# First block of a transformer trunk: three operand casts of the first turn are put in another order, and one product is issued in passes

## The chip, the cores and the metric

The kernel runs on one core of a Trainium2 chip, as one program with one launch. The metric is the device time of that program in microseconds (us); lower is better. A core has a matrix engine (PE), a vector engine (DVE), a scalar engine (ACT), GpSimd (POOL) and SyncE (SP). Each engine works through its own list of instructions in the order in which they were written, and waits on semaphores where an operand comes from another engine. Here SP starts the plain loads, and POOL starts the loads that add to what a tile holds already.

## The reference, cut to what matters

The trunk has two layers. The change lies in the very first block of the first layer, a SwiGLU feed-forward block on 512 tokens of width 1024, with 2816 hidden features:

```python
def swiglu_ffn(x, w_in, w_out):
    h = x @ w_in                       # (512, 1024) @ (1024, 5632)
    g, u = jnp.split(h, 2, axis=-1)
    return (jax.nn.silu(g) * u) @ w_out
...
x = layer_norm(a * x + 0.5 * swiglu_ffn(x, ffn_w_in[i, 0], ffn_w_out[i, 0]), ln_g[i, 0], ln_b[i, 0])
```

There are four such blocks in the program, two per layer; between them stand differential attention, a pooling mixer and two cross-attentions.

## The kernel before

**Products.** All products are made in float32 accuracy out of rounded parts: an operand is split into a high part (a cast on ACT) and a low part (source minus high part, on DVE), and a product of two split operands is three matmuls: high times high, low times high, high times low. `mm3` issues them one after the other for each block of 128 rows (lines 210, 211, 212 in the profile). `by_passes` (line 716) issues them in another order: first the sixteen matmuls that need only the high part of the weights, then the eight that need the low part.

**Seven products for eight.** The up projection works on units of 256 hidden columns. For one unit, the gate and the up half together with the two halves of the 1024 rows of the weights form a two by two block matrix; a Strassen-Winograd scheme makes it with seven block products instead of eight. The weights that these products need are sums of the blocks of `w_in`: they are made by loading a block into a buffer (`ra`, `rc`) and then letting POOL load another block on top with an adding DMA (`more`). The activations' sums ("factors") are made once per block by `second_factors`: factors 2 and 3 out of transposed x, then s2, s4 and s3, which are split into factors 4, 6 and 5 by `part`. "x's fourth sum" is s4: it becomes factor 6, the tiles `xe`.

**Units and turns.** `up` is a generator for one unit; its steps are, in order: x (factor 0), y (factor 1), z (factor 3, weights `ra` after one addition), z again (factor 6, accumulated into the same bank, weights `rd`, a second load into an `rc` buffer), then three products into x (factors 4, 5, 2). One product is 24 matmuls of 128x256. `ffn` runs three units in its first turn (lanes 0, 1, 2: first, second and third unit), calling `next` on each in a round; so the three z of factor 3 stand in a row, then the three z of factor 6, and so on. Later turns hold two units and a piece of the down projection each.

**Order.** Nothing reorders the instructions at run time: each engine's list follows the order in which the generators issue them, except where `issue_after` names an instruction that must come first; a casting instruction can then only be issued behind it. `operand(raw, behind)` does the casts of one weight block: the high part on ACT (line 689) behind `behind[0]`, the low part on DVE (line 691) behind `behind[1]`. At the start of the program (`at_start`) such ties are used because everything is short: x has to be loaded, transposed and split while the first weights land. There are four buffers each for the high (`wh`) and the low parts (`wl`) of weights; a buffer is reused when the matmuls that read it are done.

**Names in the profile.** `wh`, `wl` are weights' high and low part, `xh`, `xl`, `xe` factors' parts, `hb` and `sr` the sums before they are split, `sp` and `ha` copies of a bank that leave it free (p1, p5), `hr` the gated result. L760 and L761 are the add and the Silu on y, L772 the copy p5 of z, L125 and L126 the two instructions of `split`, L654, L656 and L661 the sums s2, s4 and s3.

Of the kernel before, what the change touches and what calls it, by code (L numbers as in the profile page):

```python
# [99 lines left out]
def drain(units):  # L100
    for _ in units:
        pass


def few(units, n):
    for _ in range(n):
        next(units, None)


class Trunk:  # L110
# [407 lines left out]
    def ffn(self, layer, j, ln, beside=()):  # L518
        w_in, w_out = self.a["ffn_w_in"][layer, j], self.a["ffn_w_out"][layer, j]
        self.seven_of, self.factors = {}, self.factor_tiles()  # L520
        nc, n, beside = self.nc, len(FFN_TURNS), iter(beside)
        at_start = bool(self.load_rest)
        downs = {i: self.down(d, w_out, 2.0 * ALPHA if i == 1 else 1.0) for i, (_, d) in enumerate(FFN_TURNS) if d}

        def start(turn):
            ups = FFN_TURNS[turn][0]

            early = (2, 1, 1) if turn == 0 else (0, 0)
            rest = self.load_rest.pop if turn == 0 and at_start else lambda: lambda: None
            got = [self.up(w_in, u, lane, early[lane], rest() if lane == 0 else None) for lane, u in enumerate(ups)]  # L530
            for lane, g in enumerate(got):
                next(g)
                if lane == 1:
                    rest()()
            if turn > 1:
                next(downs[turn])
            return got + [downs[i] for i in downs if i == turn]

        works = start(0)
        if at_start:  # L540

            zeros = self.act("hb", (P, P + S), mybir.dt.bfloat16)
            nc.vector.memset(zeros, 0.0)
            idle = self.aux("idle", "yz")
            self.warm(zeros, idle, 7)
            for tag, half in (("px", 0), ("py", 1)):
                for t in self.late[:2]:
                    self.turn(t, half, tag)
                if half == 0:
                    with self.tc.issue_after(self.last_turn.ins):  # L550
                        self.warm(zeros, idle, 9)
                next(works[0])
                if half == 0:
                    next(works[0])
            next(works[1])
        else:
            for w in works + works[:1]:
                next(w)
            self.turn_late(2)
        self.late = []  # L560
        next(works[0])
        act, dve = self.first_split
        if self.begins:

            for late, first in zip(self.begins, (act, dve)):
                self.queue_behind(late, first)
        second = self.second_factors()
        if at_start:

            next(works[0])  # L570
            for w in (works[1], second, second, works[1], works[2], works[2], works[0]):
                with self.behind():
                    next(w)
        else:
            for w in (second, *works[1:], second, downs[1]):
                next(w)
        for turn in range(n):
            behind = turn == n - 1
            for step in range(1 if turn == 0 else 0, 9 if behind else 7):
                if turn == 0 and step in (2, 3):  # L580
                    next(second)
                if step == 4:
                    if behind:
                        coming = [self.plain_down(w_out, layer, j, ln, beside)]
                    else:
                        coming = start(turn + 1)
                        if at_start and turn == 0:
                            with self.tc.issue_after(self.last_load.ins):
                                next(downs[1])
                if behind and step in (4, 6, 7, 8):  # L590
                    next(coming[0])
                if behind and step > 3:
                    few(beside, 2)

                for lane, w in enumerate(works[: None if not behind or step > 1 else -1]):
                    if not (at_start and turn == 0 and lane < 2 and step == 1):
                        next(w, None)
                if turn == 1 and step == 3:
                    self.seven_of[self.waiting[0]] = self.seven(self.waiting[1])
            works = coming  # L600
        drain(works[0])
# [13 lines left out]
    def second_factors(self):  # L615

        nc, F, H = self.nc, self.factors, 2 * P
        s1, a21, a11, a12 = (self.tmp("hb", (P, 4, H)) for i in range(4))  # L620
        s2 = self.tmp("sr", (P, 4, H))

        def sums():
            for r, (hi, lo) in zip((a11, a12), F):
                nc.vector.tensor_tensor(r, hi.bitcast(F32), lo.bitcast(F32), ALU.add)

        if self.begins is None:
            with self.tc.issue_after(self.second_split[1].ins):
                sums()

        def part(i, x, o=slice(0, H)):
            return self.split(F[i][0][:, :, o], F[i][1][:, :, o], x)

        for t in (2, 3):
            o = slice(t % 2 * P, (t % 2 + 1) * P)
            pts = []
            for half in range(2):
                pt = self.aux("pt", (("py", "yz"), ("px", "py"))[t % 2][half])
                pt = pt.rearrange("p (c n) -> p c n", c=4)
                c0 = half * S  # L640
                with self.behind():
                    self.transpose4(pt, [self.X[t][:, c0 + j * P : c0 + (j + 1) * P] for j in range(4)])
                pts.append(pt)
            nc.scalar.copy(a21[:, :, o], pts[0])
            if self.begins is None:
                self.turned_parts = part(2, pts[1], o)
            nc.vector.tensor_tensor(s1[:, :, o], pts[1], a21[:, :, o], ALU.subtract)
            self.made_parts = part(3, s1[:, :, o], o)
            if self.begins:
                part(2, pts[1], o)  # L650
            yield
        if self.begins:
            sums()
        nc.vector.scalar_tensor_tensor(s2, s1, -1.0, a11, ALU.mult, ALU.subtract)  # L654
        s4 = s1
        nc.vector.scalar_tensor_tensor(s4, s2, -1.0, a12, ALU.mult, ALU.subtract)  # L656
        part(6, s4)
        yield
        part(4, s2)
        s3 = a21  # L660
        nc.vector.tensor_tensor(s3, a11, a21, ALU.subtract)  # L661
        part(5, s3)
        yield

    def up(self, w, u, lane, early, between):
# [11 lines left out]
        def load(tag, *block):  # L677
            t = self.raw_tile((4, H), tag)
            self.last_load = nc.sync.dma_start(t, source(*block))
            return t  # L680
# [1 line left out]
        def more(t, *block):  # L682
            nc.gpsimd.dma_start(t, source(*block), accum_op=ALU.add)  # L683

        def operand(raw, behind=None):
            v = self.hl([P, 4, H])
            act, dve = behind or (None, None)
            with self.tc.issue_after(act.ins) if behind else nullcontext():
                hi = nc.scalar.copy(v[0], raw)  # L689
            with self.tc.issue_after(dve.ins) if behind else nullcontext():  # L690
                lo = nc.vector.tensor_sub(v[1], raw, v[0].bitcast(F32))  # L691
            splits.append((hi, lo))
            return v
# [28 lines left out]
        splits = []  # L722

        third = lane == 2
        at_start = early and self.begins is None
        sp = lambda: self.tmp("ha" if third else "sp", (P, 2, H))
        yz = "py" if third else "yz"
        ra = load("ra", 1, 1)
        if between:
            between()  # L730
        rc = load("rc", 2, 1)
        yield
        v = operand(ra, self.turned_parts if third and at_start else None)
        if early and lane == 0:
            self.first_split = splits[0]
        more(ra, 1, 2)
# [3 lines left out]
        if at_start and lane == 0:  # L740
            by_passes(x, v, 0, (0,))
            yield
        v2 = early > 1 and operand(rc, self.turned if at_start else None)
        if v2:
            self.second_split = splits[-1]
            yield
# [5 lines left out]
        nc.scalar.copy(p1, x)  # L752
        yield
        y = bank(self.aux("y", yz))
        v2 = v2 or operand(rc, self.made_parts if third and at_start else None)
        with self.behind() if at_start else nullcontext():
            product(y, v2, 1, True, lane != 1 and at_start)
        hr = self.tmp("hr", (P, 2, S))
# [1 line left out]
        nc.vector.tensor_tensor(h1, y, p1, ALU.add)  # L760
        nc.scalar.activation(h1, h1, AF.Silu)  # L761
        yield
        v = operand(ra, self.made_parts if at_start and lane == 0 else None)
        if at_start and lane == 0:
            self.made_parts = splits[-1]
            yield
        z = bank(self.aux("z", yz))
        product(z, v, 3, True)
        more(ra, 2, 2)
        rd = load("rc", 2, 2)  # L770
        p5 = sp()
        nc.scalar.copy(p5, z)  # L772
        yield
        product(z, operand(rd), 6)
        more(rd, 1, 2)
        yield
        product(x, operand(ra), 4)
# [911 lines left out]
```

## Time and profile before

| | |
|---|---|
| time, median of 3 runs | 1927.93 us (1924.76, 1927.93, 1930.44) |
| the profiled execution's own time | 1927.77 us |
| its span in the trace | 1926.0 us |
| PE busy | 1900.1 us, 99% of the span |
| DVE busy | 1564.4 us, 81% |
| ACT busy | 1022.8 us, 53% |
| POOL busy | 320.6 us, 17% |
| HBM traffic over the span | 143 GB/s |

The span is what the trace shows from the first to the last instruction of the profiled execution; its own time is 1.77 us longer, for what lies around it, and 0.16 us under the median of the three timed runs. A busy PE is counted from modelled ends of matmuls, so the idle times in front of single instructions and the start times tell more than the 99%. The start of the program is read in a timeline: one row for each instruction, with the start, the duration, the engine, the source line, what is written from what, and in brackets the idle time before it with what ended that.

### The profile page before, as it was taken

The numbers are of one execution on the slowest core, as the hardware profiler recorded it, in microseconds if no ns is written. First come the engines' busy times: TensorE is split into PE (matmuls) and PEld (weight loads), VectorE is DVE, ScalarE is ACT, GpSimd is POOL, SyncE is SP. The second block draws the span as 40 slices with busy tenths as digits, with TensorE's granted clock in tenths as the row PEclk, the third lists the DMA queues.
The fourth block names the chain that finished last, engine by engine and source line by source line (L and its number), as shares of the span: only waits on it lengthen the run. The fifth ranks groups of instructions, "written<-read, shape, count | busy, mean of one in ns | idle before, by whom it ended". The sixth has DMA issues, their size and how long they took to land.

```text
span 1926.0 us, 32482 instructions
## 1 busy us (share of the span) xinstructions
PE 1900.1 (99%) x13066; PEld 1741.3 (90%) x13066; DVE 1564.4 (81%) x2264; ACT 1022.8 (53%) x1580; POOL 320.6 (17%) x278
## 2 busy tenths in 40 slices
PE   9999999999999999999999999999999999999998
PEld 8999998888878888999998999999899889999997
DVE  7888989888967558888888988888887568998886
ACT  6555554567755435655554655455455436555553
POOL 2112121111210002211210321112130012111210
PEclk9999999999999999999999999999999999999999
DMA  9978772322124317978686588788344437877861
GB/s 236 220 170 184 167 141 86 91 66 88 55 99 153 110 66 192 181 175 164 139 192 179 105 179 171 176 164 186 111 132 132 132 88 157 182 160 170 184 133 56
DMA packets 246742, 277.94 MB, mean 144 GB/s; under 512 B 8256, under 2 KB 212544, under 8 KB 246592
## 3 DMA queue, kind: packets, MB, share of 16 engines
q0 software_dynamic: 92928, 92.29, 31.3%
q1 hardware_dynamic: 153664, 183.59, 29.7%
q8 instruction: 102, 1.67, 0.4%
q14 instruction: 48, 0.39, 0.1%
HBM read 273.75 MB, written 2.10 MB: 143 GB/s over the span
## 4 chain that ended last, share of the span: by engine, by line
PE 77%; DVE 14%; ACT 4%; issue 2%; DMA 2%; POOL 1%; SPq 0%; DVEq 0%; ACTq 0%; POOLq 0%
PE x L210 7%; PE x L211 7%; PE x L212 7%; PE z L212 4%; PE z L210 4%; PE z L211 4%; PE ps L210 3%; PE ps L212 3%; PE ps L211 3%; PE px L210 2%; PE px L212 2%; PE px L211 2%; PE y L212 2%; DVE wl L691 2%; PE xq L210 1%
## 5 line engine op out<-in xcount | busy, mean ns | idle before, releaser
L683 POOL DMA_DIRECT2D ra<-in_ffn_w_in_dram x132 | 171.3, 1318 | 988.9 <-DVE wl L691 812.2
L689 ACT CAST wh<-ra 128x1024 fp32r<-128x1024 f32 x176 | 185.0, 1053 | 215.6 <-PE x L211 66.6
L691 DVE TENSOR_TENSOR wl<-ra,wh 128x1024 fp32r<-128x1024 f32 x176 | 214.2, 1220 | 71.2 <-ACT wh L689 70.9
L689 ACT CAST wh<-rc 128x1024 fp32r<-128x1024 f32 x132 | 138.9, 1053 | 107.6 <-PE x L211 41.8
L210 PE MATMUL x<-xe,wh 128*128 128x256 f32 x704 | 195.2, 277 | 0.0
L211 PE MATMUL x<-xe,wh 128*128 128x256 f32 x704 | 195.1, 277 | 0.0
L212 PE MATMUL x<-xe,wl 128*128 128x256 f32 x704 | 195.0, 277 | 0.0
L125 ACT CAST wh<-b 128x1024 fp32r<-128x1024 f32 x112 | 117.8, 1052 | 132.3 <-PE x L211 65.6
L691 DVE TENSOR_TENSOR wl<-rc,wh 128x1024 fp32r<-128x1024 f32 x132 | 159.7, 1219 | 27.1 <-ACT wh L689 26.1
L126 DVE TENSOR_TENSOR wl<-b,wh 128x1024 fp32r<-128x1024 f32 x112 | 136.7, 1221 | 40.8 <-ACT wh L125 40.8
L210 PE MATMUL x<-xh,wh 128*128 128x256 f32 x536 | 148.9, 278 | 0.0
L211 PE MATMUL x<-xl,wh 128*128 128x256 f32 x536 | 148.5, 277 | 0.0
L212 PE MATMUL x<-xh,wl 128*128 128x256 f32 x536 | 148.5, 277 | 0.0
L211 PEld LDWEIGHTS x<-xe,wh 128*128 128x128 f32 x704 | 132.7, 189 | 1.4
L210 PEld LDWEIGHTS x<-xe,wh 128*128 128x128 f32 x704 | 132.2, 188 | 1.3
L212 PEld LDWEIGHTS x<-xe,wl 128*128 128x128 f32 x704 | 132.2, 188 | 0.0
L126 DVE TENSOR_TENSOR wl<-raw,wh 128x1024 fp32r<-128x1024 f32 x64 | 83.0, 1301 | 42.4 <-ACT wh L125 41.6
L211 PEld LDWEIGHTS x<-xl,wh 128*128 128x128 f32 x536 | 101.0, 189 | 0.7
L210 PEld LDWEIGHTS x<-xh,wh 128*128 128x128 f32 x536 | 100.6, 188 | 0.7
L212 PEld LDWEIGHTS x<-xh,wl 128*128 128x128 f32 x536 | 100.6, 188 | 0.0
L212 PE MATMUL z<-xe,wl 128*128 128x256 f32 x352 | 98.4, 280 | 2.2 <-DVE wl L691 2.2
L211 PE MATMUL z<-xe,wh 128*128 128x256 f32 x352 | 98.3, 279 | 0.4 <-DVE xe L126 0.4
(442 smaller groups left out, 6304.0 us busy)
## 6 DMA issues: line engine op xcount, KB each, us to landing
ra<-in_ffn_w_in_dram POOLq DMA_DIRECT2D x132, 512.0 KB, 7.0
rc<-in_ffn_w_in_dram SPq DMA_DIRECT2D x88, 512.0 KB, 5.7
b<-in_ffn_w_out_dram SPq DMA_DIRECT2D x76, 512.0 KB, 4.8
ra<-in_ffn_w_in_dram SPq DMA_DIRECT2D x44, 512.0 KB, 4.8
rc<-in_ffn_w_in_dram POOLq DMA_DIRECT2D x44, 512.0 KB, 7.9
raw<-in_xa_wkv_dram SPq DMA_DIRECT2D x16, 1024.0 KB, 5.4
raw<-in_da_w_qkv_dram SPq DMA_DIRECT2D x16, 512.0 KB, 5.3
raw<-in_xa_wq_dram SPq DMA_DIRECT2D x8, 1024.0 KB, 5.1
```

Source lines behind the costliest of these rows:

```text
L125: self.nc.scalar.copy(hi, src),
L126: self.nc.vector.tensor_sub(lo, src, hi.bitcast(F32)),
L210: mm(out, w[0], x[0], start=start, stop=False, skip_group_check=again)
L211: mm(out, w[0], x[1], start=False, stop=False, skip_group_check=again)
L212: self.last_mm = mm(out, w[1], x[0], start=False, stop=stop, skip_group_check=again)
L683: nc.gpsimd.dma_start(t, source(*block), accum_op=ALU.add)
L689: hi = nc.scalar.copy(v[0], raw)
L691: lo = nc.vector.tensor_sub(v[1], raw, v[0].bitcast(F32))
```

## The change

In the first turn of the first block (`at_start`), four things are different:

1. Lane 0 hands out an extra step for the second z: it issues the casts of `rd`, notes them in `made_parts` and yields. The loop in `ffn` takes that step (`next(works[0])`) when lane 1 has done step 2, so ahead of lane 2's z.
2. `second_factors` notes the split of s4 in `factor_parts`.
3. Lane 2's casts for its z of factor 3 are tied behind two pairs now: lane 0's `rd` casts and the split of s4. `operand` takes any number of such pairs.
4. Lane 2's z of factor 3 is issued by passes.

```diff
+                    if at_start and turn == 0 and lane == 1 and step == 2:
+                        next(works[0])
...
-        part(6, s4)
+        self.factor_parts = part(6, s4)
...
-        def operand(raw, behind=None):
+        def operand(raw, *behind):
             v = self.hl([P, 4, H])
-            act, dve = behind or (None, None)
-            with self.tc.issue_after(act.ins) if behind else nullcontext():
+            with self.after([act for act, _ in behind]):
                 hi = nc.scalar.copy(v[0], raw)
-            with self.tc.issue_after(dve.ins) if behind else nullcontext():
+            with self.after([dve for _, dve in behind]):
                 lo = nc.vector.tensor_sub(v[1], raw, v[0].bitcast(F32))
...
-        v = operand(ra, self.made_parts if at_start and lane == 0 else None)
-        if at_start and lane == 0:
+        if not at_start or lane == 1:
+            v = operand(ra)
+        elif third:
+            v = operand(ra, self.made_parts, self.factor_parts)
+        else:
+            v = operand(ra, self.made_parts)
             self.made_parts = splits[-1]
             yield
         z = bank(self.aux("z", yz))
-        product(z, v, 3, True)
+        product(z, v, 3, True, third and at_start)
         more(ra, 2, 2)
         rd = load("rc", 2, 2)
         p5 = sp()
         nc.scalar.copy(p5, z)
         yield
-        product(z, operand(rd), 6)
+        v = operand(rd)
+        if at_start and lane == 0:
+            self.made_parts = splits[-1]
+            yield
+        product(z, v, 6)
```

The other three blocks, the later turns of this one, and SP's list of loads keep their order. POOL's list changes in one place: the adding load of lane 0's `rc_484` stands ahead of that of lane 2's `ra_168` instead of behind it.

**DVE, around the s4 split, before.** `rc_484` is lane 0's `rd`, `ra_168` lane 2's weights for z, `rc_518` lane 1's `rd`; `hb_315<-sr_319,hb_318` makes s4, `xe_155` is the low part of factor 6, `xe_153` that of factor 4.

```order
L656 SCALAR_TENSOR_TENSOR hb_315<-sr_319,hb_318 128x1024
L691 TENSOR_TENSOR wl_523<-ra_168,wh_522 128x1024
L661 TENSOR_TENSOR hb_316<-hb_317,hb_316 128x1024
L126 TENSOR_TENSOR xe_155<-hb_315,xe_152 128x1024
L126 TENSOR_TENSOR xe_153<-sr_319,xe_150 128x1024
L691 TENSOR_TENSOR wl_562<-rc_484,wh_561 128x1024
L126 TENSOR_TENSOR xe_154<-hb_316,xe_151 128x1024
```

The same place of DVE now:

```order
L658 SCALAR_TENSOR_TENSOR hb_315<-sr_319,hb_318 128x1024
L692 TENSOR_TENSOR wl_523<-rc_484,wh_522 128x1024
L663 TENSOR_TENSOR hb_316<-hb_317,hb_316 128x1024
L126 TENSOR_TENSOR xe_155<-hb_315,xe_152 128x1024
L692 TENSOR_TENSOR wl_527<-ra_168,wh_526 128x1024
L126 TENSOR_TENSOR xe_153<-sr_319,xe_150 128x1024
L692 TENSOR_TENSOR wl_591<-rc_518,wh_590 128x1024
```

Lane 0's low part of `rd` has moved from fifth behind s4 to the place right behind it, and lane 2's low part has moved from there to behind the low part of factor 6.

**ACT, the same stretch, before.** `ha_416<-x_391` is lane 2's copy p1, `hr_451` its Silu, `sp_486<-z_458` and `sp_520<-z_492` the copies p5 of lanes 0 and 1.

```order
L752 COPY ha_416<-x_391 128x512
L689 CAST wh_522<-ra_168 128x1024
L689 CAST wh_561<-rc_484 128x1024
L761 ACTIVATE hr_451<-hr_451 128x2x256
L689 CAST wh_590<-rc_518 128x1024
L125 CAST xe_152<-hb_315 128x1024
L772 COPY sp_486<-z_458 128x512
L125 CAST xe_150<-sr_319 128x1024
```

And now:

```order
L753 COPY ha_416<-x_391 128x512
L690 CAST wh_522<-rc_484 128x1024
L762 ACTIVATE hr_451<-hr_451 128x2x256
L777 COPY sp_486<-z_458 128x512
L125 CAST xe_152<-hb_315 128x1024
L690 CAST wh_526<-ra_168 128x1024
L125 CAST xe_150<-sr_319 128x1024
L777 COPY sp_520<-z_492 128x512
L690 CAST wh_590<-rc_518 128x1024
```

Lane 0's cast comes first; lane 2's has gone from the first place behind p1 to behind lane 0's p5 and the high part of factor 6; lane 1's has gone behind lane 1's p5.

**PE, where lane 2's z of factor 3 (`z_530`) passes over to lane 0's z of factor 6 (`z_458`), now.** Before, the 24 matmuls of lane 2's product went in threes, each with `wl` as the third.

```order
L717 MATMUL z_530<-xh_85,wh_526 128x256
L717 MATMUL z_530<-xl_87,wh_526 128x256
L210 MATMUL z_458<-xe_152,wh_522 128x256
L717 MATMUL z_530<-xh_85,wl_527 128x256 x8
L211 MATMUL z_458<-xe_155,wh_522 128x256
L212 MATMUL z_458<-xe_152,wl_523 128x256
```

The eight matmuls with the low part now stand at the end of lane 2's product, behind the first matmul of lane 0's.

More of the change, by code (lines that the diff above doesn't have):

```diff
@@ L724, in up @@
         third = lane == 2
-        at_start = early and self.begins is None
+        at_start = early > 0 and self.begins is None
         sp = lambda: self.tmp("ha" if third else "sp", (P, 2, H))
@@ L732, in up @@
         yield
-        v = operand(ra, self.turned_parts if third and at_start else None)
+        v = operand(ra, *((self.turned_parts,) if third and at_start else ()))
         if early and lane == 0:
@@ L742, in up @@
             yield
-        v2 = early > 1 and operand(rc, self.turned if at_start else None)
+        v2 = early > 1 and operand(rc, *((self.turned,) if at_start else ()))
         if v2:
@@ L754, in up @@
         y = bank(self.aux("y", yz))
-        v2 = v2 or operand(rc, self.made_parts if third and at_start else None)
+        v2 = v2 or operand(rc, *((self.made_parts,) if third and at_start else ()))
         with self.behind() if at_start else nullcontext():
```

## The prediction

> **What bounds the kernel now.** I read the page first, for what is scarce over the whole span.
>
> ```profile
> PE 1900.1 (99%) x13066; PEld 1741.3 (90%) x13066; DVE 1564.4 (81%) x2264; ACT 1022.8 (53%) x1580; POOL 320.6 (17%) x278
> ```
>
> PE is the bound almost everywhere, so the change, which leaves out no work, can only give back time in which PE stands still or runs slowly, and only in the first turn of the first block, where it moves something. So next come the waits of PE over the first 130 us.
>
> ```profile
> PE z L212 <- DVE wl L691: 2.2, 1, 2.2
> PE z L211 <- DVE xe L126: 0.4, 1, 0.4
> ```
>
> Both stand at one place, the passage from the third unit's z (factor 3) to the first unit's z (factor 6). The timeline of PE there:
>
> ```profile
> 34.74 0.28 PE L210 MATMUL z<-xh,wh 128*128 128x256 f32 x1
> 35.15 0.38 PE L212 MATMUL z<-xh,wl 128*128 128x256 f32 x1
> 37.75 0.36 PE L210 MATMUL z<-xe,wh 128*128 128x256 f32 x1
> 38.51 0.38 PE L211 MATMUL z<-xe,wh 128*128 128x256 f32 x1 [0.40 <-DVE xe L126]
> 41.07 0.53 PE L212 MATMUL z<-xe,wl 128*128 128x256 f32 x1 [2.17 <-DVE wl L691]
> 41.40 0.42 PE L210 MATMUL z<-xe,wh 128*128 128x256 f32 x1
> 45.28 0.28 PE L210 MATMUL z<-xe,wh 128*128 128x256 f32 x1
> 48.00 0.28 PE L210 MATMUL z<-xe,wh 128*128 128x256 f32 x1
> ```
>
> The last two rows are the first matmuls of the second and the third unit's product: 24 matmuls in 48.00 - 45.28 = 2.72 us, 0.113 us each, undisturbed. The third unit's z took 37.75 - 34.74 = 3.01, which is 0.29 too long. The first unit's z of factor 6 took 45.28 - 37.75 = 7.53, which is **4.81** too long. Of that, 3.09 is waiting (its third matmul at 41.07 instead of 37.75 + 0.23 = 37.98) and 1.72 is slowness: from 41.40 on a matmul takes about 0.21 us. Two stretches of the busy-time table, with the granted clock third from the right, say why.
>
> ```profile
> 37.74:41.15 3.41, 0.83 (x5) 0.44 (x3) 3.21 (x4) 3.41 (x5) 0.00 (x0) 1.00 1.04 159
> 41.15:44.57 3.42, 3.42 (x16) 3.42 (x17) 3.42 (x4) 1.27 (x2) 2.04 (x2) 0.50 0.33 33
> ```
>
> After 3.41 us in which PE was busy for 0.83, the clock was granted at 0.50 for the next 3.42. So 0.29 + 4.81 = **5.10 us** is all that this place can give back. There is no other idle PE before 130 us that the change touches.
>
> Who makes PE wait is seen in the other engines' timelines. ACT:
>
> ```profile
> 27.80 0.57 ACT L752 COPY ha<-x 128x512 f32<-128x512 f32 x1
> 32.78 1.05 ACT L689 CAST wh<-ra 128x1024 fp32r<-128x1024 f32 x1 [4.41 <-DMA ra<-in_ffn_w_in_dram]
> 33.74 1.05 ACT L689 CAST wh<-rc 128x1024 fp32r<-128x1024 f32 x1
> 36.16 1.04 ACT L125 CAST xe<-hb 128x1024 fp32r<-128x1024 f32 x1
> 37.10 0.57 ACT L772 COPY sp<-z 128x512 f32<-128x512 f32 x1
> 37.58 1.04 ACT L125 CAST xe<-sr 128x1024 fp32r<-128x1024 f32 x1
> ```
>
> DVE:
>
> ```profile
> 30.91 1.22 DVE L656 SCALAR_TENSOR_TENSOR hb<-sr,hb 128x1024 f32<-128x1024 f32 x1
> 33.87 1.23 DVE L691 TENSOR_TENSOR wl<-ra,wh 128x1024 fp32r<-128x1024 f32 x1 [1.74 <-ACT wh L689]
> 37.23 1.22 DVE L126 TENSOR_TENSOR xe<-hb,xe 128x1024 fp32r<-128x1024 f32 x1 [1.01 <-ACT xe L125]
> 38.65 1.23 DVE L126 TENSOR_TENSOR xe<-sr,xe 128x1024 fp32r<-128x1024 f32 x1 [0.20 <-ACT xe L125]
> 39.80 1.22 DVE L691 TENSOR_TENSOR wl<-rc,wh 128x1024 fp32r<-128x1024 f32 x1
> ```
>
> ACT stood idle for 4.41 us for the third unit's accumulated weights, with the first unit's cast queued behind it, and then both engines made everything at once: the low part that PE waited for ended at 39.80 + 1.22 = 41.02.
>
> **The change part by part.** The new order is followed through with these durations. On a full engine the next large cast starts 0.95 after the last (ACT, 32.78 to 33.74), a small copy takes 0.48 of the queue (37.10 to 37.58), and a large DVE operation 1.15 at most (38.65 to 39.80), from which the times below are reckoned with 1.14.
>
> *The first unit's `rd` casts, moved ahead.* The high part can start when the load has landed. The issue in the window around 13.9 us, the lane 0 `rd`, and the time to landing:
>
> ```profile
> 13.90 0.37 SPq L679 DMA_DIRECT2D rc<-in_ffn_w_in_dram x1
> ...
> rc<-in_ffn_w_in_dram SPq DMA_DIRECT2D x1, 512.0 KB, 13.1
> ```
>
> It lands at 27.0, and its new `wh` buffer was last read by the third unit's x, long done. So the cast runs from about 28.3 to 29.3, in the idle time of ACT. On DVE the low part goes behind s4 (30.91), from 32.05 to 33.27. Both lie beside PE's z products of the first two units, at no cost: PE needs them at 37.5. What now stands behind the cast on ACT is the third unit's Silu, the first unit's p5 and the s4 split; the cover is 1.9 us, since p5 cannot start before the first unit's z ends.
>
> ```profile
> 31.91 0.28 PE L212 MATMUL z<-xh,wl 128*128 128x256 f32 x1
> ```
>
> *The s4 split, moved ahead.* p5 starts at about 32.23 (that matmul ends at 32.19), the high part of factor 6 at 32.71, until 33.75 (s4 itself is there at 32.13). On DVE: s3 from 33.18, then the low part from 34.32 to 35.54, where before it ended at 38.45. PE needs it at about 37.6. The 0.40 us wait is gone.
>
> *The third unit's casts, moved back.* They are what pays. The high part, now behind the split, starts at 33.67 instead of 32.78 and ends at 34.72. PE wants it at 34.74, when the second unit's z is issued. How PE takes up work after a cast is seen earlier in its timeline, where the cast ended at 26.42:
>
> ```profile
> 26.47 0.38 PE L716 MATMUL y<-xh,wh 128*128 128x256 f32 x1 [0.48 <-ACT wh L689]
> 26.69 0.28 PE L716 MATMUL y<-xl,wh 128*128 128x256 f32 x1
> ```
>
> 0.05 after the cast, and 0.11 lost on the first step. So PE starts at 34.77 and loses up to 0.14. The low part runs from 35.46 to 36.68 on DVE.
>
> *z by passes.* The 24 matmuls stay 24, but the low part is wanted only after 16 of them and the one of `z_458`, at 34.77 + 0.1 + 17 x 0.113 = 36.8, so 36.68 is in time by 0.1, where in threes it would have been wanted at 35.0. The 0.29 of before is gone; if DVE is late by d, d - 0.1 is lost.
>
> *What follows.* The third unit's `rd` is issued, and lands after, as these rows say:
>
> ```profile
> 28.15 0.37 SPq L679 DMA_DIRECT2D rc<-in_ffn_w_in_dram  x1
> ...
> rc<-in_ffn_w_in_dram SPq DMA_DIRECT2D x1, 512.0 KB, 7.6
> ```
>
> The first unit's z of factor 6 ends at about 40.3. The second unit's `rd` parts are made by 37.1 and 39.0, wanted at 40.3; the third's, landed at 35.75 and cast at 38, by 39.0 and 41.25, wanted at 43.0. The added waits of lane 2's casts hold back nothing that is wanted earlier than these. POOL's adding loads of the `rc` buffers are issued earlier, since their casts are; that of lane 0 goes ahead of that of lane 2's `ra`, behind a low part that is there at 33.3 instead of 41.0.
>
> *The sum.* Removed 5.10, added between 0 and 0.6 (0.14 for the start, the rest if both engines run half a microsecond behind this reckoning); I take 0.1, next to the reckoned row. The profiled execution's own time was 1927.77, so 1927.77 - 5.0 = **1922.8 us**, against the median of 1927.93 a saving of 0.26%. A measurement of this kernel can tell about 0.3%, 5.8 us, from no change.
>
> **The rivals.** *The slow clock was an accident of that execution.* The clock fell after a stretch of 3.41 us with little work, and where such stretches begin may differ between executions. The longest other single wait of PE, 1.36 us in the attention, left no trace in the granted clock, which is 1.00 all around it:
>
> ```profile
> 380.03 0.33 PE L494 MATMUL pt<-ident,p 128*128 128x128 f32 x1 [1.36 <-DVE p L1130]
> ...
> 376.00:392.00 16.00, 14.64 (x113) 13.96 (x113) 14.93 (x47) 10.63 (x29) 2.36 (x3) 1.00 0.13 44
> ```
>
> Here PE had two waits with one matmul between, some 2.6 us idle; cut by a border between two stretches, it might not have slowed PE, and then most executions before lost only 0.29 + 3.09 = 3.4. The gain is 3.3 and the time 1924.5. For it: the fastest of three runs is 3.2 under the median. Against: the profiled execution, with its slow stretch, lies at the median.
> [...]
>
> *The transfers keep their times.* The DMA engines are full up to the stall and nearly empty in it (second number from the right).
>
> ```profile
> 39.00:41.00 2.00, 0.00 (x0) 0.00 (x0) 2.00 (x3) 2.00 (x4) 0.00 (x0) 1.00 1.05 165
> 41.00:43.00 2.00, 1.93 (x9) 1.93 (x10) 2.00 (x3) 1.42 (x2) 1.28 (x1) 0.54 0.06 9
> ```
>
> If they stay full behind it, loads may land no earlier though PE is. The two casts that waited for a transfer later in this turn, and when PE wanted them:
>
> ```profile
> 65.19 1.05 ACT L689 CAST wh<-ra 128x1024 fp32r<-128x1024 f32 x1 [1.45 <-DMA ra<-in_ffn_w_in_dram]
> 71.38 1.05 ACT L689 CAST wh<-ra 128x1024 fp32r<-128x1024 f32 x1 [3.15 <-DMA ra<-in_ffn_w_in_dram]
> ```
>
> ```profile
> 72.48 0.28 PE L210 MATMUL x<-xh,wh 128*128 128x256 f32 x1
> 77.92 0.28 PE L210 MATMUL x<-xh,wh 128*128 128x256 f32 x1
> ```
>
> With PE 5.0 earlier they are wanted at 67.5 and 72.9. High parts end at 66.2 and 72.4, low parts 1.2 later, and those are wanted 0.2 after the start: no wait at the first, some 0.5 at the second. The gain would be 4.5 and the time 1923.3. It is unlikely in full, because the transfers paused for these two microseconds, at a share of 0.06, and now have something to do there.
>
> *Slower: the first unit's `rd` lands late and stands in front of everything on ACT.* The cast now heads ACT's list. If the load lands at T instead of 27.0, p5, the s4 split and the third unit's casts move by T - 30.7 as soon as T is over 30.7, and PE waits that long at 34.74, once more with a slow stretch of 1.7 behind it. The whole gain is used up from T = 34.0 on, and 1927.77 + 5.8 needs T near 40. For it: loads of this stretch take 7.6 to 13.1 us to land, all different. Against is the slowest load in the chain of waits, the third unit's first `rc`:
>
> ```profile
> 8.76 16.53 DMA rc<-in_ffn_w_in_dram
> ```
>
> With its 16.5 us T would be 30.4, just under the border; and nothing ahead of 27 us has moved. T at 40 gives about 1933.7.
>
> **How the numbers follow.** The forecast, -5.0, gets 0.78; the accident of the clock 0.11; the transfers 0.06; the late `rd` 0.05. The three runs lie within 5.7 us, so two medians differ by two or three microseconds by themselves: of the forecast, which is 0.8 short of the bound of 5.8, some two fifths (0.33) come out faster by over 0.3%; of the accident 0.03 and of the transfers 0.02. That is 0.38 faster; 0.05 slower, the late `rd` alone; the rest, 0.57, within 0.3%. The range goes from 1922.8 - 3.2 (the fastest run's distance from the median) = 1919.6 to the clock rival's 1924.5 with 2.0 of spread, 1926.5.
>
> **What would show it.** Right: no wait of PE over 0.2 us between 30 and 45 us; granted clock 1.00 throughout; the first unit's product of factor 6 ends near 40.3; ACT's first `rc` cast at 28.3; the product that began at 72.48 begins near 67.5. Wrong in size: a wait for `wh` at 34.7 or for `wl` at 36.8, or ACT waiting for a transfer after 60 us with PE idle behind it. Wrong altogether: ACT idle until after 30.7 for the first unit's `rd`, or a stretch at 0.50 somewhere else.

## The result and the profile after

The changed kernel takes **1923.05 us** (median of 13 runs, 1920.70 to 1926.82); the kernel before, run beside it, 1927.33 us (13 runs, 1924.76 to 1930.44). The ratio is 0.998 with a 95% interval of 0.9972 to 0.9989: 4.3 us less, with 2.1 to 5.4 inside the interval. The forecast was 1922.8. The execution that was profiled was the slowest of the 13: its own time is 1926.82, its span 1923.9 us. So places are compared here, not spans.

The waits of PE over the first 130 us of the changed kernel (in all, times, longest):

```profile
PE x L717 <- ACT wh L690: 1.3, 1, 1.3
PE idle L120 <- DVE hb L543: 1.2, 1, 1.2
PE y L717 <- ACT wh L690: 0.3, 1, 0.3
PE x L717 <- DVE wl L692: 0.3, 1, 0.3
```

There is no z among them any more. The same view of the kernel before has three waits beside the two z that the prediction showed:

```profile
PE idle L120 <- DVE hb L543: 1.3, 1, 1.3
PE y L716 <- ACT wh L689: 0.5, 1, 0.5
PE x L716 <- ACT wh L689: 0.2, 1, 0.2
```

So the waits that are left are of the kind that was there before. All four are earlier than the place in question. The first, at 24.00 us, is long in this execution, in which a load of weights came late (the cast that PE waited for began at 22.90, after ACT had stood idle for 2.19 us until that load, and in the profile of before at 21.22 without such a wait; in two more traces of this kernel the wait of PE is 0.2 us at most), and it is why everything below is some 1.45 us later than foretold. PE's timeline, from the third unit's z of factor 3 to the second unit's z of factor 6 and that of the third:

```profile
36.23 0.38 PE L717 MATMUL z<-xh,wh 128*128 128x256 f32 x1
36.45 0.28 PE L717 MATMUL z<-xl,wh 128*128 128x256 f32 x1
...
38.21 0.28 PE L210 MATMUL z<-xe,wh 128*128 128x256 f32 x1
38.40 1.22 PE L717 MATMUL z<-xh,wl 128*128 128x256 f32 x8
...
42.16 0.28 PE L210 MATMUL z<-xe,wh 128*128 128x256 f32 x1
...
44.99 0.28 PE L210 MATMUL z<-xe,wh 128*128 128x256 f32 x1
```

I call the time from the first of these rows to the row at 42.16 the **passage**: the 48 matmuls of two products, undisturbed 48 x 0.1133 = 5.44 us. Where PE's list mixes the products, the first 48 matmuls from the third unit's z on are counted, whichever product they belong to. It took 5.93 us here and 45.28 - 34.74 = 10.54 us in the profile of before. The busy-time table at the same place, with the granted clock third from the right:

```profile
33.58:36.99 3.41, 3.41 (x31) 3.36 (x30) 3.41 (x4) 3.31 (x4) 1.34 (x2) 1.00 1.15 189
36.99:40.41 3.42, 3.42 (x30) 3.31 (x30) 3.42 (x4) 3.42 (x6) 1.28 (x1) 1.00 1.24 197
40.41:43.82 3.41, 3.41 (x32) 3.41 (x31) 3.41 (x4) 2.52 (x4) 1.93 (x2) 1.00 1.24 198
```

PE and DVE are both busy throughout, and the clock stays at 1.00. ACT works in the new order, the first unit's `rd` (29.52) ahead of the split of s4 (34.17) and the third unit's weights (35.12), and without holes from the split on:

```profile
29.52 1.05 ACT L690 CAST wh<-rc 128x1024 fp32r<-128x1024 f32 x1
...
33.69 0.59 ACT L777 COPY sp<-z 128x512 f32<-128x512 f32 x1 [0.35 <-PE z L212]
34.17 1.05 ACT L125 CAST xe<-hb 128x1024 fp32r<-128x1024 f32 x1
35.12 1.05 ACT L690 CAST wh<-ra 128x1024 fp32r<-128x1024 f32 x1
```

and so does DVE (first unit's low part, the sum s3, low part of factor 6, third unit's low part):

```profile
33.72 1.22 DVE L692 TENSOR_TENSOR wl<-rc,wh 128x1024 fp32r<-128x1024 f32 x1
34.85 1.22 DVE L663 TENSOR_TENSOR hb<-hb 128x1024 f32<-128x1024 f32 x1
35.99 1.22 DVE L126 TENSOR_TENSOR xe<-hb,xe 128x1024 fp32r<-128x1024 f32 x1
37.13 1.21 DVE L692 TENSOR_TENSOR wl<-ra,wh 128x1024 fp32r<-128x1024 f32 x1
```

### The profile page after: what moved, and what is told of

It reads as the page before. It is cut to its first block, busy times and chain, and to the rows that moved or that the text cites. A ratio compares the mean times of both kernels' runs of the same rounds, so it can differ in the third digit from the quotient of the medians.

```text
span 1923.9 us, 32479 instructions
## 1 busy us (share of the span) xinstructions
PE 1899.5 (99%) x13066; PEld 1741.6 (91%) x13066; DVE 1563.9 (81%) x2264; ACT 1023.3 (53%) x1580; POOL 319.6 (17%) x278
## 4 chain that ended last, share of the span: by engine, by line
PE 78%; DVE 13%; ACT 4%; DMA 2%; issue 2%; POOL 1%; SPq 0%; DVEq 0%; ACTq 0%; POOLq 0%
PE x L210 7%; PE x L211 7%; PE x L212 7%; PE z L212 4%; PE z L210 4%; PE z L211 4%; PE ps L210 3%; PE ps L212 3%; PE ps L211 3%; PE px L210 2%; PE px L212 2%; PE px L211 2%; PE x L717 2%; PE y L212 2%; PE xq L210 2%
## 5 line engine op out<-in xcount | busy, mean ns | idle before, releaser
L125 ACT CAST wh<-raw 128x1024 fp32r<-128x1024 f32 x64 | 66.5, 1049 | 59.4 <-PE xq L211 21.2
```

The costliest lines, as they stand in the source:

```text
L125: self.nc.scalar.copy(hi, src),
```

## Experiments

The questions were: is it this place that pays; which part of the change pays; did the slow clock belong to the stall or to one execution; and would a late `rd` have cost what the rival said. Each run gives the passage from its trace, and most a time against the kernel before on the same chip. In g1 and g3, where PE stands still ahead of the passage, it is counted from the end of the second unit's last matmul instead, which makes it some 0.17 us shorter than the others' way of counting.

| kernel | passage, us | clock at it | time, us | before beside it |
|---|---|---|---|---|
| changed (three traces) | 5.93, 5.60, 5.78 | 1.00 | 1923.05 | 1927.33 |
| before (three traces) | 10.54, 11.59, 10.05 | 0.50 for 3.4, 6.8, 3.4 us | 1927.33 | |
| e1, `rd` first alone, with passes | 5.65 | 1.00 | 1924.20 | 1927.36 |
| e2, casts without passes | 5.98 | 1.00 | 1923.67 | 1927.36 |
| e3, passes alone | 10.40 | 0.50 for 3.4 us | 1927.64 | 1927.36 |
| e4, the wait filled | 8.43 | 1.00 | 1926.19 | 1927.36 |
| g2, tie to s4 and passes | 7.23 | 1.00 | 1924.94 | 1926.65 |
| g1, `rd` late | 7.02 | 1.00 | 1924.49 | 1926.65 |
| g3, `rd` later | 15.10 | 0.50 for 6.8 us | 1931.38 | 1925.76 |

**e1: the first unit's `rd` casts ahead, third unit's casts not tied to s4.** From the changed kernel:

```diff
-            v = operand(ra, self.made_parts, self.factor_parts)
+            v = operand(ra, self.made_parts)
```

> Measure D: from the first matmul of the third unit's z (factor 3) to the first matmul of the second unit's z of factor 6; 10.54 us in the trace before, 5.93 in the trace of the change, 5.44 without any stall. Here lane 0's rd casts stay ahead, and z stays in passes, but lane 2's casts are no longer tied behind the split of s4. Theory (the first unit's low part was late, and its move is what pays): the third unit's casts run first, the low part of factor 6 ends near 37.5, just when PE wants it, so D is 5.4 to 6.2, and the second unit's low part may cost another 0.5 one product later; time within 1 us of the changed kernel (1923). Rival (the tie behind s4 is what pays): D of 8 or more, time near 1926.

The passage, again from the third unit's z to the second unit's z of factor 6:

```profile
35.90 0.28 PE L717 MATMUL z<-xh,wh 128*128 128x256 f32 x1
...
41.55 0.28 PE L210 MATMUL z<-xe,wh 128*128 128x256 f32 x1
```

5.65 us, no wait, and not even the short start at the third unit's first matmul (0.28 where the changed kernel has 0.38); its cast is no longer tied behind the split of s4. The ratio to before is 0.9983 (0.9975 to 0.9992). The time of 1924.20 is 1.2 us over that of the changed kernel, where 1 was allowed, but the intervals of the two gains overlap. So the tie to s4, which moves the third unit's casts further back, adds nothing that can be seen once `rd` is ahead.

**e2: the casts in the new order, z not by passes.** From the changed kernel:

```diff
-        product(z, v, 3, True, third and at_start)
+        product(z, v, 3, True)
```

> All casts as in the changed kernel, but the third unit's z goes in threes again. Theory: its first low part is wanted 0.23 us after the start and comes about 1.9 us after it (DVE 35.46 to 36.68 in the reckoning), so PE waits about 1.7 us inside this product and D is 7.2 without a slow stretch of the clock, up to 8.9 with one; time 1.7 to 3.4 us over the changed kernel. Rival (passes do nothing that counts): D under 6.2 and the same time as the changed kernel.

The passage was 5.98 us, and I had expected 7.2, because in threes the low part is wanted from the third matmul on. The timeline shows what became of that wait:

```profile
34.21 0.39 PE L210 MATMUL z<-xh,wh 128*128 128x256 f32 x1
34.44 0.28 PE L211 MATMUL z<-xl,wh 128*128 128x256 f32 x1
34.55 0.28 PE L210 MATMUL z<-xe,wh 128*128 128x256 f32 x1
34.96 0.38 PE L211 MATMUL z<-xe,wh 128*128 128x256 f32 x1
```

After two matmuls of the third unit's z (`xh`, `xl`) PE's list goes on with eleven matmuls of the first unit's z (`xe`), and comes back at 36.22. It seems that the build puts ready work of another product ahead of a matmul whose operand it expects late. So the statement that each list follows the generators' order but for the named ties is too strong: the order that runs is not always the one in which the source issues. The ratio is 0.9976 (0.9966 to 0.9986), as good as with passes.

**e3: passes alone.** From the kernel before:

```diff
-        product(z, v, 3, True)
+        product(z, v, 3, True, third and bool(at_start))
```

> Order of the casts as before, the third unit's z by passes. Theory: only the 0.29 us inside that product goes, PE reaches the first unit's product of factor 6 0.29 earlier and waits as much longer, since its low part still ends near 41.0: D is 10.5 with a slow stretch of the clock, 8.8 without; time as before within 1 us. Rival (passes pay by themselves): D 2 us shorter or more, at an equal clock.

PE's waits between 30 and 45 us are those of before, and the clock fell behind them:

```profile
PE z L212 <- DVE wl L691: 2.2, 1, 2.2
PE z L211 <- DVE xe L126: 0.4, 1, 0.4
...
37.55:40.96 3.41, 1.16 (x7) 0.96 (x8) 3.21 (x4) 3.41 (x6) 0.30 (x1) 1.00 0.88 139
40.97:44.38 3.41, 3.41 (x18) 3.41 (x17) 3.41 (x4) 0.57 (x2) 2.42 (x3) 0.50 0.53 72
```

The ratio is 1.0 (0.9991 to 1.0009): without the casts the passes bring nothing. What PE waits for last comes as late as ever: the matmul with the first unit's low part starts 7.22 us after DVE begins the third unit's (40.19 and 32.97), and before 7.20 (41.07 and 33.87).

**e4: the wait filled.** The kernel before, with twenty matmuls put in the long wait; they go to a bank that nobody reads:

```diff
         product(z, v, 3, True)
+        if at_start and third:
+            idle = bank(self.aux("idle", "py"))
+            for _ in range(20):
+                nc.tensor.matmul(
+                    idle[:, 0], v[0][:, 0, :P], self.factors[3][0][:, 0], start=True, stop=True
+                )
```

> The kernel before with 20 more matmuls of 128x256 (into a bank that nobody reads) between the third unit's z and the first unit's product of factor 6: PE is busy through most of its wait, which stays. Theory (the slow clock came from PE's idleness and cost 1.72 us of the 4.81): the matmul that waits for the low part still starts near 41.07, the clock stays at 1.00, D is 41.07 - 34.74 + 22 x 0.113 = 8.8; time 1 to 2 us under the kernel before. Rival (the slow clock is no matter of this idleness): a stretch at 0.50 in spite of it, and D of 10 or more.

```profile
37.99 2.43 PE L772 MATMUL idle<-xh,wh 128*128 128x256 f32 x20
41.07 0.39 PE L212 MATMUL z<-xe,wl 128*128 128x256 f32 x1 [0.43 <-DVE wl L691]
43.70 0.28 PE L210 MATMUL z<-xe,wh 128*128 128x256 f32 x1
```

The matmul with the low part starts at 41.07 as in the profile of before (to the hundredth by chance: in f3 and f4 it is 40.44 and 40.73), but the product behind it runs at full clock and ends 1.58 us earlier (43.70 for 45.28). One trace could have missed the stretch, but the mean clock of all eleven runs says the same (below). So in this case it was the idle PE that the clock fell behind, not the place or the operands: the same place with the wait filled kept 1.00, where before, e3, f3 and f4 had 0.50. The ratio is 0.9993 (0.9984 to 1.0002), which cannot be told from no change; the 1.2 us between the medians has the size that a slow stretch in some executions would give, but is not shown.

**f1 to f4: the changed kernel twice, the kernel before twice more**, one trace each, for the question whether the slow stretch was an accident.

> The changed kernel once more, for a second trace. Theory (the matmuls' spacing takes one of two values, 0.113 or 0.118 us for 128x256, set anew by a wait and kept until the next, by chance of the execution): D (first matmul of the third unit's z to the first of the second unit's z of factor 6) without a stall, 5.4 to 6.0; granted clock 1.00; the spacing between 40 and 140 us may be 0.118 as in the first trace or 0.113, and the time goes with it, by some 4 us between the two. Rival (the new order itself makes the slow spacing): 0.118 from 36 to 144 us again.

> As the run before it: a third trace of the changed kernel. Theory: no stall at the z products, clock 1.00, spacing by chance; rival: 0.118 from 36 to 144 us in each trace of it.

> The kernel before once more. Theory (the slow clock follows from the idle PE, wherever the stretches of 3.41 us begin): two waits of 0.4 and 2.2 us and one stretch at 0.50 behind them, D 10.3 to 10.6. Rival (the slow clock was an accident of the first execution): waits of the same length, but clock 1.00 and D about 8.8. On the spacing, theory of chance: 0.113 or 0.118 from 45 to 140 us; rival: 0.113 as in the first trace.

> As the run before it: a third trace of the kernel before. Theory: waits of 0.4 and 2.2 us, a stretch at 0.50, D 10.3 to 10.6; rival: clock 1.00 and D about 8.8.

The changed kernel passed in 5.60 and 5.78 us at a clock of 1.00, the kernel before in 11.59 and 10.05, on either side of the 10.3 to 10.6 expected. Their single times are 1922.61, 1923.79, 1926.96 and 1927.67 us. The busy-time table of f3 shows the stretch twice as long:

```profile
36.30:39.72 3.42, 1.58 (x12) 1.17 (x10) 2.92 (x3) 3.42 (x6) 0.00 (x0) 1.00 1.19 180
39.72:43.13 3.41, 2.69 (x12) 2.69 (x13) 3.41 (x4) 2.07 (x3) 1.28 (x1) 0.50 0.21 26
43.12:46.53 3.41, 3.41 (x18) 3.41 (x17) 1.89 (x3) 1.04 (x1) 3.34 (x3) 0.50 1.12 172
```

All four traces of kernels that keep the stall (before, e3, f3, f4) have it. But the runs without a trace say more. Each run lists its mean granted clock to three digits: 0.999 in every one of the eight traces without a slow stretch, 0.998 in the three with one of 3.4 us, 0.997 in the two with 6.8 us (f3, g3). By that mark, of 62 runs of the kernel before (30 beside e1 to e4, 19 beside g1 and g2, 13 beside g3) **35 had the slow stretch and 27 had not**; of e3's eleven, seven had it; of all 65 runs of the kernels without the long wait, none. The mark is sharp enough: the eight traces lie between 0.9987 and 0.9994, and one stretch takes off half of 3.41 us in 1926, 0.0009, so a run with one lies at 0.9978 to 0.9985. So the stretch belongs to the stall, but comes in somewhat over half of the executions.

An estimate from the traces' rows gives about half too. It assumes, which no run shows, that the clock goes by the number of matmuls that start in a stretch of 3.41 us, the length of the slow stretches. The stretches of 3.41 us before the clock fell held the starts of 3 matmuls (before), 6 (f4), 7 (e3) and 9 (f3); with 11 (g3, below) and 15 (g1) it did not fall. Lay stretches of 3.41 us over the stall of before, where matmuls start every 0.113 us but between 37.75 and 41.29 only at 38.51 and 41.07. Let the borders fall anywhere with equal chance: then 0.57 of the positions have a stretch with nine starts or fewer. The stalls of e3, f3 and f4 give 0.58, 0.54 and 0.50, and with ten starts as the border it is 0.57 to 0.64. Counted were 35 of 62, or 0.56.

**g2: the tie to s4 and the passes, `rd` not ahead.** From the kernel before:

```diff
-        part(6, s4)
+        self.factor_parts = part(6, s4)
...
-        v = operand(ra, self.made_parts if at_start and lane == 0 else None)
+        v = operand(ra, self.made_parts if at_start and lane == 0 else self.factor_parts if at_start and third else None)
...
-        product(z, v, 3, True)
+        product(z, v, 3, True, third and bool(at_start))
```

> The kernel before with the third unit's casts tied behind the split of s4, and its z of factor 3 by passes; the first unit's rd casts stay where they were. Theory (the first unit's rd casts ahead are what pays): DVE makes s4, s3, the low part of factor 6, the third unit's low part and then factors 4 and 5 before the first unit's low part of rd, which PE gets at 38.9 to 41; the wait for wl stays at 1.3 to 2.5 us, D is 7.5 to 10.5 and the time within 2.5 us of the kernel before. Rival (moving the third unit's casts back is what pays, as the prediction said): D under 6.5 and the time 3.5 to 5 us under the kernel before.

```profile
38.39 0.39 PE L210 MATMUL z<-xe,wh 128*128 128x256 f32 x1 [0.33 <-ACT wh L689]
38.61 0.28 PE L211 MATMUL z<-xe,wh 128*128 128x256 f32 x1
39.33 0.38 PE L210 MATMUL z<-xe,wh 128*128 128x256 f32 x1 [0.44 <-ACT wh L689]
39.55 0.28 PE L211 MATMUL z<-xe,wh 128*128 128x256 f32 x1
39.91 0.39 PE L212 MATMUL z<-xe,wl 128*128 128x256 f32 x1
```

Neither expectation holds as written. The passage, 7.23, is a little under the 7.5 to 10.5 of the one and over the 6.5 of the other: with the split of s4 first, `xe` no longer comes late, the two first pairs of the first and second unit's z are put into the wait for `wl`, and 7.23 - 5.44 = 1.8 us are left, spread over short waits for two high parts and the low part. The clock stays at 1.00, and no run of the ten has the mark of a slow stretch. The ratio is 0.999 (0.9981 to 0.9999). So the tie with the passes removes about two thirds of the 5.10 us, the slow stretch and about half of the waiting, and the `rd` casts ahead with the passes (e1) remove all of it. The `rd` casts ahead with neither the tie nor the passes were not run.

**g1 and g3: the first unit's `rd` late.** The changed kernel with that load started from ACT's queue, in g1 behind the third unit's copy p1 and in g3 behind its Silu. The edit of g3:

```diff
-        nc.scalar.activation(h1, h1, AF.Silu)
+        silu = nc.scalar.activation(h1, h1, AF.Silu)
+        if at_start and third:
+            self.third_silu = silu
...
-        rd = load("rc", 2, 2)
+        late = at_start and lane == 0
+        rd = None if late else load("rc", 2, 2)
...
+        if late:
+            rd = self.raw_tile((4, H), "rc")
+            with self.tc.issue_after(self.third_silu.ins):
+                nc.scalar.dma_start(rd, source(2, 2))
```

> The changed kernel, but the first unit's rd load is started from ACT's queue behind the third unit's copy p1 (about 28.3 us) instead of from SP's at 13.9, so that it lands late (T, about 36 to 37). Theory (the price of the rival that ended slower): its cast heads ACT's list, p5, the split of s4 and the third unit's casts stand behind it, PE waits for the third unit's high part from 35 to about T + 4 = 40 or 41; D (the first matmul of the third unit's z of factor 3 to that of the second unit's z of factor 6) does not show this, so it is taken from the end of the second unit's z of factor 3: that to the second unit's z of factor 6 is about 11 to 12 us and 1.7 to 3.4 more for a slow clock, where it is 5.7 in the changed kernel and 10.0 to 11.6 in the kernel before; time 1929 to 1934, so 2 to 6 us over the kernel before. Rival (it does not matter what stands in front of ACT's list, since the scheduler puts other work ahead of a cast that waits): this stretch under 8 us and the time 1922 to 1926.

> The changed kernel, but the first unit's rd load is started from ACT's queue behind the third unit's Silu, which waits for DVE, so at about 32; it lands at T of about 38. With so late a load the build puts the split of s4 and both copies p5 ahead of that cast in ACT's list; the third unit's casts stay tied behind it. Theory (a late load costs what it delays the third unit's casts, and from some T on more than the change brings): the third unit's high part ends at about T + 2.1 = 40.3, PE waits 5 us for it (but for two matmuls of the first unit's second z) and runs at a clock of 0.50 for 3.4 to 6.8 us behind that, which costs 1.7 to 3.4; the stretch from the end of the second unit's z of factor 3 to the second unit's z of factor 6 is 11 to 14.5 us, and the time 1929 to 1932, 2 to 5 us over the kernel before. Rival (such waits are made up for elsewhere, or the gain is not this stretch at all): the time stays under 1926.

In g1 the load landed sooner than meant. Its issue is tied behind the copy p1 in ACT's list, but it stands at 26.89 and the copy began only at 28.30, so it did not wait for the copy to be carried out. The issue, ACT's cast of the load, PE's first matmul of the third unit's z, and two stretches of the busy-time table:

```profile
26.89 0.41 ACTq L785 DMA_DIRECT2D rc<-in_ffn_w_in_dram  x1
...
33.10 1.05 ACT L690 CAST wh<-rc 128x1024 fp32r<-128x1024 f32 x1 [4.23 <-DMA rc<-in_ffn_w_in_dram]
...
37.09 0.39 PE L717 MATMUL z<-xh,wh 128*128 128x256 f32 x1 [1.46 <-ACT wh L690]
...
34.10:37.52 3.42, 1.96 (x17) 1.76 (x16) 3.34 (x3) 3.42 (x6) 1.28 (x1) 1.00 1.18 235
37.52:40.93 3.41, 3.41 (x32) 3.41 (x31) 3.41 (x4) 3.41 (x5) 1.28 (x1) 1.00 1.24 198
```

T is 33.05 instead of 36 to 37, so the expected 11 to 12 us could not come. PE starts 3.99 after the cast began; the prediction's rule for it, 34.74 + T - 30.7, gives T + 4.04 = 37.09. The wait of 1.46 brought no slow stretch, in the trace or by the mark in any of the ten runs. The passage counted from the end of the second unit's z (37.09 - 1.46 = 35.63) is 42.65 - 35.63 = 7.02, and the ratio is 0.9987 (0.9978 to 0.9997): 2.2 us of the gain are left. These are the numbers of the rival expectation, but not for its reason: nothing was put ahead of the cast, and ACT stood idle for 4.23 us in front of it. In g3:

```profile
40.65 1.04 ACT L690 CAST wh<-rc 128x1024 fp32r<-128x1024 f32 x1 [4.99 <-DMA rc<-in_ffn_w_in_dram]
...
41.75 0.58 PE L210 MATMUL z<-xe,wh 128*128 128x256 f32 x1 [6.71 <-ACT wh L690]
...
33.62:37.03 3.41, 1.43 (x13) 1.23 (x11) 2.42 (x2) 1.95 (x3) 0.00 (x0) 1.00 1.19 265
37.03:40.45 3.42, 0.00 (x0) 0.00 (x0) 0.00 (x0) 0.00 (x0) 0.00 (x0) 0.99 0.78 129
40.45:43.86 3.41, 1.95 (x7) 1.66 (x8) 2.13 (x2) 3.21 (x4) 0.61 (x1) 0.50 0.01 1
```

The load landed at 40.6 instead of the 38 meant, PE stood still for 6.71 us, and the clock was at half for 6.8 us from 40.4 on; the passage is 50.14 - (41.75 - 6.71) = 15.10, and the time 1931.38 us, **5.6 us over the kernel before** beside it (ratio 1.0026, 1.0016 to 1.0036). Both are a little over the expected 11 to 14.5 and 2 to 5, as the load was later. So the same order of casts is a gain or a loss by the time at which one load lands.

## Why the prediction was right, and where it was not

*The place and its cover.* Right. The predicted steps, against f1, whose start was undisturbed: ACT's `rd` cast 28.3, measured 28.25; p5 32.23, 32.39; the split of s4 32.71, 32.87; the third unit's cast 33.67, 33.82; PE's start 34.77, 35.02; its first matmul with the low part wanted at 36.8, run at 36.98; second unit's z of factor 6 at about 40.3, 40.62. In the profile first shown the same steps are all 1.2 to 1.9 later for the wait at 24.00, and no wait of PE stands between 30 and 45 us. The loss in that profile was 0.22 - 0.118 = 0.10 at the start, 0.19 - 0.118 = 0.07 before the low part and 1.05 - 8 x 0.118 = 0.11 in the eight matmuls with it, 0.28 together (5.93 against 48 x 0.118 = 5.66); in f1 it was 5.60 - 5.44 = 0.16. The prediction took 0.1 out of 0 to 0.6. One reading of it does not fit its own border: it gave the cover behind the `rd` cast as 1.9 us, but from a start at 28.3 to the border of 30.7 it is 2.4, and in f1 ACT's idle times there are 1.99 and 0.47, 2.46 together.

*The size of what is removed.* The waiting, 0.29 + 3.09, is gone. **The step that was mis-sized is the 1.72 us for the slow clock.** It was put in whole, and the accident got 0.11; in fact both are so, each in part of the executions: 35 of 62 runs had the stretch, which is a mean of 0.56 x 1.71 = 0.96. Then 3.38 + 0.96 - 0.1 gives 4.2, and 4.3 was measured between the medians. This sum fits, but is not shown in all its terms: among the runs of before, those with the stretch were on average only 0.6 us longer (standard error 0.4) than those without, not 1.7. Whatever makes up the rest in the others was not traced, since every traced execution of before had the stretch. That the time of 1922.8 came within 0.3 us of 1923.05 is partly luck: a gain of 5.0 was forecast and 4.3 measured, and the forecast was counted from an execution of 1927.77, 0.4 over the median of the thirteen. Nor did the clock fall at one place of the stall: it fell at 41.15 us in before, 40.97 in e3, 39.72 in f3 and 41.39 in f4, where the first matmul with the first unit's low part starts at 41.07, 40.19, 40.44 and 40.73, and of the 3.41 us ahead of the fall PE had been busy for 0.83, 1.16, 1.58 and 1.04.

*What pays.* Wrong. The prediction said of the third unit's casts, moved back, that they are what pays, and gave the passes a role of their own. e1 shows the first unit's `rd` casts ahead, with the passes, to be enough; the tie to s4 with the passes leaves 1.8 us of waiting (g2); the passes alone give nothing (e3), and without them the gap is filled with other matmuls (e2). The passes can't be called useless, only unnecessary here.

*The transfers.* They did move: the casts that waited for a load at 65.19 and 71.38 stand at

```profile
62.68 1.05 ACT L690 CAST wh<-ra 128x1024 fp32r<-128x1024 f32 x1 [1.54 <-DMA ra<-in_ffn_w_in_dram]
68.65 1.05 ACT L690 CAST wh<-ra 128x1024 fp32r<-128x1024 f32 x1 [2.70 <-DMA ra<-in_ffn_w_in_dram]
```

and in f1 at 61.23 and 67.24, 4.0 and 4.1 earlier. PE has no wait behind them, and the product that began at 72.48 begins at 67.82 in f1, where 67.5 was foretold.

*The late `rd`.* It did not happen in any trace of the changed kernel, but its mechanism is real. At T = 33.05 the rule for PE's start was exact; the wait was 1.46 instead of T - 30.7 = 2.35, since PE came to it later than 34.74, and the slow stretch that the prediction put behind it did not come. At T = 40.6 it overstates: by it PE would have waited 40.6 - 30.7 = 9.9 us, and it waited 6.71, because with that load the build put the split of s4 and the copies p5 ahead of the cast on ACT, so that only one cast lay between `rd` and the third unit's weights. The rival's time for T = 40 was 1933.7, 5.8 over the kernel before; 5.6 over was measured. That this fits is partly luck: PE waited 3.2 us less than by the rule, but worked at half clock from 41.75 to 47.2, which by my estimate (half of these 5.45 us) costs some 2.7 us where 1.7 was reckoned.

## What to carry to other kernels

Where an engine idles for one operand with casts queued behind, look first for a cast that is ready and needed soon, and put it into that idle time; that alone may be the whole gain. Before such a cast is put at the head of a list, note when its load lands and how much later it may land: here the margin was 3.7 us (27.0 against 30.7), the gain half gone at 33 and a loss of 5.6 us at 40.6. A short stall of PE may cost more than its length by the clock behind it (here 3.09 us of waiting had 3.42 us at 0.50 behind them in the profile of before, reckoned at 1.72 us), but count that part by how many executions show it (here 35 of 62), not by the one that was profiled.

## What the chip showed that I had not expected

*When the clock falls.* A stretch of 3.41 us in which PE was busy for 1.58 was followed by one at 0.50 (f3), one with 1.96 by none (g1), and one with 1.43 (g3) by none yet; there the clock fell only behind the empty stretch that came next (0.00 busy from 37.03 to 40.45). So modelled busy time does not put the three in order. The count of matmuls that start in the stretch does: 9 in f3, 11 in g3, 15 in g1, of some 30 that find room in 3.41 us; with so few cases this is no rule yet. (The x in a row counts also those that began before the stretch and reach into it. In g1, where no fall marks where to count from, the stretch from 34.10 is taken, which holds the whole wait.) A stretch at half clock in which PE was busy for 2.69 of 3.41 was followed by a second one (f3).

*Two paces at one clock.* PE's matmuls of 128x256 start 0.113 or 0.118 us apart at a granted clock of 1.00. The passage's last rows above give (44.99 - 42.16) / 24 = 0.118 for the execution first shown; f1, the same kernel, ran

```profile
40.62 0.28 PE L210 MATMUL z<-xe,wh 128*128 128x256 f32 x1
...
43.34 0.28 PE L210 MATMUL z<-xe,wh 128*128 128x256 f32 x1
```

at 2.72 / 24 = 0.113. Ten products on, this alone is 1.07 us (42.16 to 70.43 against 40.62 to 67.82). It is one part of why the profiled execution of the changed kernel is later than f1, beside the late start. The new order does not set the pace, since f1 is the same kernel; nor does a wait alone, since in f1 the change from 0.118 to 0.113 comes at 35.26, inside the third unit's product and without a listed wait. What sets it stays open.
